# State-space scan: decay matrices written over their rows, rows fetched one head pair ahead, four DRAM copies of the rows instead of sixteen

## The chip, the cores and the metric

The kernel runs on one core of a Trainium2 chip. The metric is device time in microseconds, the median of the runs of one program. Of the core's engines the text speaks of TensorE (PE, matmuls; PEld is its weight load), VectorE (DVE), ScalarE (ACT), GpSimd (POOL) and SyncE (SP). SP computes nothing here: it issues nearly all transfers, one after the other, and a transfer whose target buffer is not free yet holds up everything behind it on SP. The transfers themselves are carried by 16 DMA engines.

## What is computed

The reference is an encoder of two layers on 512 tokens of width 1024. Each layer is a half-step feed-forward block, a token mixer and a second half-step feed-forward block, with layer norms between. The mixer of the first layer is a state-space mixer (Mamba-2 SSD) run in both directions; the change is in that mixer alone.

```python
proj = u @ w_in                       # z, xbc, dt_raw
xbc = silu(depthwise_conv(xbc, conv_w, conv_b))
dt = softplus(dt_raw + dt_bias);  A = -exp(a_log)
# per direction, 32 heads of 64 columns, 4 groups of B and C:
a_cs = cumsum(dt * A);  L = exp(segsum(a))          # decay matrix, per head
y_diag = einsum(C @ B^T, L, X * dt)
y_off  = C @ state * exp(a_cs)                      # what earlier tokens left
y = (y_f + y_b + X * d_skip) * silu(z);  y = rms_per_group(y) * norm_g
out = y @ w_out
```

## The kernel before

All matrix products in float32 are split into high and low parts and done as three matmuls; one *unit* is a 128x1024 block of weights (512 KB), loaded by SP into a `raw` buffer (`load`, L99), split by ACT (L123, `wh`) and DVE (L124, `wl`), and used by 24 matmuls of 512 columns (L166).

The state-space mixer is the function `ssm`. Its decay matrix for a head is exp(row + bias), where the row is the same for all 128 partitions and the bias is a column. So each head needs three rows of 512 numbers, spread over all partitions. `dt_chain` computes all rows once, as tiles `rows` and `rowe`, and writes them to a DRAM tile `scr` of shape [16, 32, 3, 512]: 16 equal copies of 32 heads times three rows (L667). `ssd_head` (one head) then fetches from it with two transfers: `rw`, two rows (L761, 128x1024, 512 KB in the tile), and `ch`, the third row (L763, 256 KB). The source pattern is 16 copies outermost, each read 8 times, so that partitions 0 to 7 get copy 0 and so on.

With `rw` there, POOL masks it (`mask`, L778) in place and into a second tile `dx`; `ssd_mats` makes the matrices of half of the tokens (`c` = 0 or 1): four exponentials on ACT (L786 to L789) into a tile `E` and into `dx`, an addition on POOL (L792) and a multiplication by `cb` on DVE (L793). DVE multiplies `ch` by C (L764). `ssd_out` then runs on PE (L803): for two heads, four products with `E` and two with `ch` for each half. In the trace each of these is two instructions, so a half is 8 and 4.

Two heads are a *pair*; there are 16 pairs, 4 in each of 4 groups, and each pair has two halves. Between the halves the main loop puts *units* of other work: the projections of the next group (`bc`, `x`), the gate (`z`) and the output projection of the group before (`wso`). Before the first group, `prepare` turns the group's B, C and x into the tiles `bt`, `cb`, `xt`, `st`.

Buffers: `rw` two, `E` five (which `dt_chain` also uses for its temporaries), `dx` two, `ch` three, `raw` four. The program is written in one order, and a scheduling layer arranges it for each engine by its own estimates of durations. Once built, the order on each engine is fixed, and an engine waits at its next instruction whatever stands behind it.

Of the kernel before, what the change touches and what calls it, by code (L numbers as in the profile page):

```python
# [9 lines left out]
F32 = mybir.dt.float32  # L10
F32R = mybir.dt.float32r
AF = mybir.ActivationFunctionType
ALU = mybir.AluOpType

P = 128
T = 512
# [2 lines left out]
FT = 22  # L19
FPARTS = (8, 7, 7)  # L20
NA = 32
NE = 5
NG = 4
NST = 128
ALPHA = 4.0 ** 0.25
EPS = 1e-5
# [20 lines left out]
def hybrid_trunk(tc, xT, cb, par, cst, adaw, wgu, wdn0, wdn1, wdn2, wdt, win, wso, wqk, wv, wao, dist_in, dtp, lam_in, out):  # L47
    nc = tc.nc
# [540 lines left out]
    def ssm(n):  # L589
        u = next_u[0]  # L590
        sc = ExitStack()
        ep = sc.enter_context(tc.tile_pool(name="ep", bufs=2))
# [6 lines left out]
        W = 256  # L599
        bias = ep.tile([P, 4, 64], F32, name="ssbias", bufs=1)  # L600
        dd = ep.tile([P, 4, 32], F32, name="dd", bufs=1)
        scr = dp.tile([16, 32, 3, T], F32, name="scr")

        def dt_proj():
            w = split(load(wdt, 512))
# [5 lines left out]
        def dt_chain(pd):  # L611
            dtT = tmp("dtT")
            nc.scalar.activation(dtT[:64], pd[:64], AF.Copy)
            pt = acc("ln")
            for i in range(4):
                nc.tensor.transpose(pt[:, i * 64 : (i + 1) * 64], dtT[:64, i * P : (i + 1) * P], ident[:64, :64])
            e1, e2, e3 = (ep.tile([P, T], F32, tag="E", name="E", bufs=NE) for _ in range(3))
            v, q, e, uu, lu = e1[:, :W], e1[:, W:], e2[:, :W], e2[:, W:], e3[:, :W]
            nc.vector.tensor_tensor(out=v, in0=pt[:, :W], in1=dtc[:, :W], op=ALU.add)
            nc.vector.scalar_tensor_tensor(out=q, in0=v, scalar=-1.0, in1=v, op0=ALU.mult, op1=ALU.max)  # L620
            nc.scalar.activation(e, q, AF.Exp, scale=-1.0)
            ea = e3[:, W:]
            nc.scalar.activation(ea, dtc[:, W:], AF.Exp)
            nc.vector.tensor_scalar(out=v, in0=v, scalar1=0.0, scalar2=None, op0=ALU.max)
            nc.vector.tensor_scalar(out=uu, in0=e, scalar1=1.0, scalar2=None, op0=ALU.add)
            nc.scalar.activation(lu, uu, AF.Ln)
            nc.vector.tensor_scalar(out=uu, in0=uu, scalar1=1.0, scalar2=None, op0=ALU.subtract)
            nc.vector.tensor_tensor(out=uu, in0=e, in1=uu, op=ALU.subtract)
            nc.vector.tensor_scalar(out=e, in0=e, scalar1=-0.5, scalar2=1.0, op0=ALU.mult, op1=ALU.add)
            nc.vector.tensor_tensor(out=uu, in0=uu, in1=e, op=ALU.mult)  # L630
            nc.vector.tensor_tensor(out=lu, in0=lu, in1=uu, op=ALU.add)
            nc.vector.tensor_tensor(out=v, in0=v, in1=lu, op=ALU.add)
            at = q
            nc.vector.scalar_tensor_tensor(out=at, in0=v, scalar=-1.0, in1=ea, op0=ALU.mult, op1=ALU.mult)
            nc.vector.tensor_scalar(out=v, in0=v, scalar1=1e-37, scalar2=None, op0=ALU.max)
            nc.scalar.activation(lu, v, AF.Ln)
            pcs = acc("ln")
            nones = tmp("nones")[:, :P]
            nc.gpsimd.memset(nones, -1.0)
            plan = {  # L640
                (0, 0): [(sgt, 0), (nones, 1)], (0, 1): [(sgt, 1)],
                (0, 2): [(sle, 2)], (0, 3): [(ones, 2), (sle, 3)],
                (1, 0): [(sge, 0), (ones, 1)], (1, 1): [(sge, 1)],
                (1, 2): [(slt, 2)], (1, 3): [(nones, 2), (slt, 3)],
            }
            for (dr, i), lst in plan.items():
                for k, (mk, j) in enumerate(lst):
                    nc.tensor.matmul(
                        pcs[:, i * 64 + dr * 32 : i * 64 + dr * 32 + 32], lhsT=mk,
                        rhs=at[:, j * 64 + dr * 32 : j * 64 + dr * 32 + 32],  # L650
                        start=k == 0, stop=k == len(lst) - 1,
                    )
            cs = tmp("cs")[:, :W]
            nc.scalar.activation(cs, pcs[:, :W], AF.Copy)
            nc.vector.tensor_tensor(out=bias.rearrange("p i h -> p (i h)"), in0=lu, in1=cs, op=ALU.subtract)
            pr = acc("ln")
            for i in range(4):
                nc.tensor.transpose(pr[:64, i * P : (i + 1) * P], cs[:, i * 64 : (i + 1) * 64], ident)
            rows = big(name="rows")
            nc.scalar.activation(rows[:64], pr[:64], AF.Copy)  # L660
            rowe = big(name="rowe")
            nc.scalar.activation(rowe[32:64, :W], pr[32:64, :W], AF.Exp)
            nc.scalar.activation(rowe[0:32, W:], pr[0:32, W:], AF.Exp)
            nc.scalar.activation(dd[:, 0:2, :], bias[:, 0:2, 0:32], AF.Exp)
            nc.scalar.activation(dd[:, 2:4, :], bias[:, 2:4, 32:64], AF.Exp)
            for j, a, b, src in ((0, 0, T, rows[0:32]), (1, 0, T, rows[32:64]), (2, 0, W, rowe[32:64]), (2, W, T, rowe[0:32])):
                nc.sync.dma_start(  # L667
                    scr[:, :, j, a:b].rearrange("r h x -> h r x"), src[:, a:b].unsqueeze(1).broadcast_to([32, 16, b - a])
                )

        last_in, last_exp = [None], [None]
# [44 lines left out]
        def prepare(g, xs, bc):  # L716
# [37 lines left out]
                states.append(st)  # L754
            return xt, cbs, states, Ct

        def ssd_head(h, Ct):

            src = scr[:, h].unsqueeze(1)
            rw = ep.tile([P, 2, T], F32, tag="rw", name="rw")  # L760
            nc.sync.dma_start(rw, src[:, :, 0:2].broadcast_to([16, 8, 2, T]))  # L761
            ch = ep.tile([P, T], F32, tag="ch", name="ch", bufs=3)
            nc.sync.dma_start(ch, src[:, :, 2].broadcast_to([16, 8, T]))  # L763
            nc.vector.tensor_tensor(out=ch, in0=ch, in1=Ct, op=ALU.mult)  # L764
            dx = ep.tile([P, 2, 2, P], F32, tag="dx", name="dx")
            f4 = rw[:, 0, :].rearrange("p (c o q) -> p c o q", c=2, o=2)
            b4 = rw[:, 1, :].rearrange("p (c o q) -> p c o q", c=2, o=2)
            for o, i_, fwd in (
                (f4[:, :, 0, :], f4[:, :, 0, :], True), (b4[:, :, 1, :], b4[:, :, 1, :], False),
            ):  # L770
                mask(o, i_, fwd)
            for o in range(2):
                mask(dx[:, :, o, :], (b4 if o == 0 else f4)[:, :, o, :], o == 1, inplace=False)
            return rw, ch, dx
# [6 lines left out]
            )  # L781

        def ssd_mats(h, c, rw, dx, cbs):
            E = ep.tile([P, T], F32, tag="E", name="E", bufs=NE)
            i = 2 * c
            nc.scalar.activation(E[:, :W], rw[:, 0, c * W : (c + 1) * W], AF.Exp, bias=bias[:, i, h : h + 1])  # L786
            nc.scalar.activation(E[:, W:], rw[:, 1, c * W : (c + 1) * W], AF.Exp, bias=bias[:, i + 1, 32 + h : 33 + h])
            nc.scalar.activation(dx[:, c, 0, :], dx[:, c, 0, :], AF.Exp, bias=bias[:, i, 32 + h : 33 + h])
            e = nc.scalar.activation(dx[:, c, 1, :], dx[:, c, 1, :], AF.Exp, bias=bias[:, i + 1, h : h + 1])  # L789
            last_exp[0] = e if h < 24 else None  # L790
            dg = E.rearrange("p (k q) -> p k q", k=4)[:, 0:4:3, :]
            nc.gpsimd.tensor_tensor(out=dg, in0=dg, in1=dx[:, c], op=ALU.add)  # L792
            nc.vector.tensor_tensor(out=E, in0=E, in1=cbs[c], op=ALU.mult)  # L793
            return E

        def ssd_out(pr_, c, py, mats, chs, xt, states):
            cc = slice(c * W, (c + 1) * W)
            col = [slice(pr_ * P + hh * 64, pr_ * P + (hh + 1) * 64) for hh in range(2)]
            for k in range(3):
                for hh in range(2):  # L800
                    lhs = xt[2 * c + k][:, col[hh]] if k < 2 else states[1 - c][:, col[hh]]
                    rhs = mats[hh][:, k * W : (k + 1) * W] if k < 2 else chs[hh][:, cc]
                    nc.tensor.matmul(py[hh * 64 : (hh + 1) * 64, cc], lhsT=lhs, rhs=rhs, start=k == 0, stop=k == 2)  # L803

        def gated_norm(g, ys, zs):
# [28 lines left out]
        def run(units):  # L834
            for f in units:
                f()
# [5 lines left out]
        run(units_x(0, xs, cols=HALVES)[:2])  # L842
        dt_chain(pd)
        run(units_x(0, xs)[2:])
        silu(bc + xs)
        scale_residual()
        run(units_z(0, zs[0])[:2])
# [9 lines left out]
        for g in range(NG):  # L857
# [7 lines left out]
            for s in range(8):  # L865
                pr_, c = divmod(s, 2)
                ft = g * 4 + pr_
                if c == 0:
                    heads = [ssd_head(ft * 2 + hh, Ct) for hh in range(2)]
                    py = acc("mid")  # L870
                mats = [ssd_mats(ft * 2 + hh, c, heads[hh][0], heads[hh][2], cbs) for hh in range(2)]
                ssd_out(pr_, c, py, mats, [hd[1] for hd in heads], xt, states)
                if c == 1:
                    nc.vector.scalar_tensor_tensor(
                        out=xs[pr_], in0=xs[pr_], scalar=pc(C_D + ft), in1=py, op0=ALU.mult, op1=ALU.add
# [321 lines left out]
```

## Time and profile before

| | |
|---|---|
| median of three runs | 2179.48 us (2178.3 to 2181.34) |
| the profiled execution's own time | 2176.88 us |
| its span, first to last instruction | 2174.8 us |
| PE busy | 97% |
| DVE busy | 82% |
| ACT, POOL busy | 50%, 7% |
| moved by DMA | 301.18 MB, mean 138 GB/s |
| the scan of the state-space mixer, first to last product of `ssd_out` | about 458 to 766 us |

Times are microseconds from the start of the span. A busy PE is not PE at its peak, since matmuls overlap; what counts are the stretches in which PE has nothing to do. A view of waits names the engine that waited, the line and tile of the waiting instruction, what it waited for, the total, the number of times and the longest. A row of the timeline has start, duration, engine, line, operation, output and inputs, count, and in brackets the idle time ahead of it. A row of stretches has, for each engine, busy time and instructions, then the granted clock of PE, the share of time in which the DMA engines were busy, and GB/s.

### The profile page before, as it was taken

How to read it: one execution, taken by the hardware profiler on the slowest of the kernel's cores; microseconds unless marked ns; L12 is line 12 of the kernel's file. 1: busy time of each engine (PE TensorE's matmuls, PEld its weight loads, DVE VectorE, ACT ScalarE, POOL GpSimd, SP SyncE). 2: the span in 40 equal slices, each digit the busy share in tenths (PEclk: the TensorE clock that was granted, in tenths of full speed). 3: DMA queues.
4: the chain of work that ended last, by engine and by line, in shares of the span. 5: the costliest groups of instructions: out<-in, count | busy, mean ns of one | idle time of the engine just before them, and what ended most of it. 6: DMA issues, size and time to landing. Idle time of an engine off the chain costs nothing.

```text
span 2174.8 us, 34198 instructions
## 1 busy us (share of the span) xinstructions
PE 2119.9 (97%) x13206; PEld 1859.7 (86%) x13206; DVE 1775.3 (82%) x3086; ACT 1092.4 (50%) x1828; POOL 154.2 (7%) x258
## 2 busy tenths in 40 slices
PE   7999999999999989999999999999999989999997
PEld 6889899866777778999999989899888869989897
DVE  6979899556766689989889998987877879858697
ACT  4424354767655546434356534343866637424353
POOL 0000000045232300000000000000111100000000
PEclk9999999999999999999999999999999989999999
DMA  9863644464535423646443273723322212323231
GB/s 324 302 212 121 219 138 149 123 183 137 158 123 155 121 68 126 214 144 198 159 132 105 97 261 96 254 94 111 98 80 79 76 59 78 127 69 117 84 110 39
DMA packets 90082, 301.18 MB, mean 138 GB/s; under 512 B 10048, under 2 KB 13504, under 8 KB 89920
## 3 DMA queue, kind: packets, MB, share of 16 engines
q1 hardware_dynamic: 88384, 294.81, 41.7%
q0 software_dynamic: 1536, 4.20, 0.9%
q8 instruction: 103, 1.69, 0.3%
q14 instruction: 59, 0.48, 0.1%
HBM read 289.53 MB, written 5.24 MB: 136 GB/s over the span
## 4 chain that ended last, share of the span: by engine, by line
PE 59%; DVE 3%; issue 2%; ACT 2%; POOL 1%; DMA 0%; POOLq 0%; ACTq 0%; DVEq 0%; SPq 0%
PE acc L166 47%; PE mid L166 9%; PE mid L965 1%; PE ln L166 1%; PE ln L987 0%; DVE resid L278 0%; DMA raw<-in_wgu 0%; DVE resid L320 0%; PE ln L253 0%; PE ln L302 0%; ACT p L975 0%; POOL E L792 0%; ACT wh L123 0%; PE ln L1004 0%; DVE p L968 0%
## 5 line engine op out<-in xcount | busy, mean ns | idle before, releaser
L166 PE MATMUL acc<-hi,wh 128*128 128x256 f32 (+1 forms) x1592 | 533.1, 336 | 9.2 <-DVE resid L372 7.1
L166 PE MATMUL acc<-hi,wl 128*128 128x256 f32 (+1 forms) x1592 | 532.6, 335 | 0.0
L166 PE MATMUL acc<-lo,wh 128*128 128x256 f32 (+1 forms) x1592 | 532.1, 335 | 0.1
L166 PE MATMUL acc<-uh,wh 128*128 128x256 f32 (+1 forms) x1160 | 391.2, 338 | 0.0
L166 PE MATMUL acc<-ul,wh 128*128 128x256 f32 (+1 forms) x1160 | 389.6, 336 | 0.0
L166 PE MATMUL acc<-uh,wl 128*128 128x256 f32 (+1 forms) x1160 | 388.9, 336 | 0.0
L123 ACT ACTIVATE wh<-raw 128x1024 fp32r<-128x1024 f32 (+1 forms) x210 | 212.8, 1021 | 277.5 <-PE acc L166 95.4
L166 PEld LDWEIGHTS acc<-hi,wh 128*128 128x128 f32 x1592 | 302.9, 190 | 45.5 <-DVE resid L372 6.6
L470 ACT ACTIVATE wh<-raw 128x1024 fp32r<-128x1024 f32 x198 | 209.1, 1059 | 259.4 <-DVE raw L480 129.1
L166 PEld LDWEIGHTS acc<-lo,wh 128*128 128x128 f32 x1592 | 302.9, 190 | 31.0 <-DVE lo L154 1.3
L166 PEld LDWEIGHTS acc<-hi,wl 128*128 128x128 f32 x1592 | 303.0, 190 | 30.3 <-issue 0.5
L124 DVE TENSOR_TENSOR wl<-raw,wh 128x1024 fp32r<-128x1024 f32 (+1 forms) x210 | 248.4, 1185 | 46.7 <-ACT wh L123 45.4
L471 DVE TENSOR_TENSOR wl<-raw,wh 128x1024 fp32r<-128x1024 f32 x198 | 240.8, 1219 | 38.9 <-ACT wh L470 38.1
L166 PEld LDWEIGHTS acc<-uh,wh 128*128 128x128 f32 x1160 | 219.0, 189 | 28.6 <-issue 6.2
L166 PEld LDWEIGHTS acc<-ul,wh 128*128 128x128 f32 x1160 | 219.3, 189 | 25.1 <-issue 3.2
L166 PEld LDWEIGHTS acc<-uh,wl 128*128 128x128 f32 x1160 | 219.2, 189 | 23.7 <-issue 2.4
L480 DVE TENSOR_TENSOR raw<-raw 128x512 f32<-128x512 f32 x264 | 181.3, 688 | 5.0
L184 DVE SCALAR_TENSOR_TENSOR raw<-raw,cond 128x1024 f32<-128x1024 f32 x144 | 174.1, 1218 | 9.9 <-DMA raw<-in_adaw 9.7
L372 DVE SCALAR_TENSOR_TENSOR resid<-acc,gv,resid 128x512 f32<-128x512 f32 (+1 forms) x166 | 109.4, 663 | 58.8 <-PE acc L166 58.4
L316 POOL TENSOR_TENSOR rr<-vr,mhalf 128x2 f32<-128x2 f32 x12 | 8.4, 698 | 1527.6 <-DVE vr L312 1527.6
L166 PE MATMUL mid<-uh,wh 128*128 128x256 f32 (+2 forms) x332 | 99.8, 302 | 0.0
L166 PE MATMUL mid<-uh,wl 128*128 128x256 f32 (+2 forms) x332 | 99.3, 299 | 0.0
(266 smaller groups left out, 3920.7 us busy)
## 6 DMA issues: line engine op xcount, KB each, us to landing
raw<-in_wgu SPq DMA_DIRECT2D x176, 512.0 KB, 4.2
raw<-in_adaw SPq DMA_DIRECT2D x144, 512.0 KB, 4.6
raw<-in_wdn SPq DMA_DIRECT2D x64, 448.0 KB, 4.0
raw<-in_win SPq DMA_DIRECT2D x40, 512.0 KB, 4.2
raw<-in_wdn SPq DMA_DIRECT2D x32, 512.0 KB, 4.4
rw<-scr SPq DMA_DIRECT2D x32, 512.0 KB, 5.5
ch<-scr SPq DMA_DIRECT2D x32, 256.0 KB, 3.6
raw<-in_wso SPq DMA_DIRECT2D x16, 512.0 KB, 3.5
```

Of the source, the lines that this page charges most:

```text
L123: nc.scalar.activation(hi[:, :n], raw, AF.Copy)
L124: nc.vector.tensor_tensor(out=lo[:, :n], in0=raw, in1=hi[:, :n].bitcast(F32), op=ALU.subtract)
L166: last = nc.tensor.matmul(o, lhsT=a, rhs=b, start=start and j == 0, stop=j == n - 1, skip_group_check=not start)
L184: nc.vector.scalar_tensor_tensor(out=raw, in0=raw, scalar=1.0, in1=cond, op0=ALU.mult, op1=ALU.mult, accum_out=mods[l][:, j : j + 1],)
L316: nc.gpsimd.tensor_tensor(out=r[:, :m], in0=vr[:, :m], in1=mhalf[:, :m], op=ALU.pow)
L372: nc.vector.scalar_tensor_tensor(out=res[d][:, a:b], in0=pd[:, a:b], scalar=gvec[n][:, d : d + 1], in1=res[d][:, a:b], op0=ALU.mult, op1=A ...
L470: nc.scalar.activation(x[0], r, AF.Copy)
L471: nc.vector.tensor_tensor(out=x[1], in0=r, in1=x[0].bitcast(F32), op=ALU.subtract)
L480: nc.vector.tensor_tensor(out=o, in0=x, in1=y, op=ALU.add)
L965: nc.tensor.matmul(ss[m], lhsT=q[:, c], rhs=qks[h, 1][m], start=j == 0, stop=j == 1)
```

## The change

- The tile `E` goes. `ssd_mats` writes the exponentials over the rows in `rw`, and the addition and multiplication work there too; `ssd_out` reads its matrices from `rw`. A row tile is thus held until the pair's last product and not only until its last exponential.
- `rw` has six buffers (`NRW`), and `dt_chain` takes two of them for its temporaries.
- The fetch of `rw` moves out of `ssd_head` into `fetch(ft)`, which the main loop calls for the next pair at the start of a pair, and for the first pair right behind the x projections of the first group. `ch` is fetched where it was.
- `scr` has 4 copies (`NREP`): L667 writes a quarter as much, and the source pattern of `rw` and `ch` is 4 copies outermost, each read 32 times.

```diff
-NE = 5
+NRW = 6
+NREP = 4
...
-        scr = dp.tile([16, 32, 3, T], F32, name="scr")
+        scr = dp.tile([NREP, 32, 3, T], F32, name="scr")
...
-            e1, e2, e3 = (ep.tile([P, T], F32, tag="E", name="E", bufs=NE) for _ in range(3))
+            e12, e3 = (ep.tile([P, 2, T], F32, tag="rw", name="ew", bufs=NRW) for _ in range(2))
+            e1, e2, e3 = e12[:, 0, :], e12[:, 1, :], e3[:, 0, :]
...
-                    scr[:, :, j, a:b].rearrange("r h x -> h r x"), src[:, a:b].unsqueeze(1).broadcast_to([32, 16, b - a])
+                    scr[:, :, j, a:b].rearrange("r h x -> h r x"), src[:, a:b].unsqueeze(1).broadcast_to([32, NREP, b - a])
...
+        rows_of = {}
+
+        def fetch(ft):
+            if ft >= 16:
+                return
+            for h in (2 * ft, 2 * ft + 1):
+                rw = ep.tile([P, 2, T], F32, tag="rw", name="rw", bufs=NRW)
+                nc.sync.dma_start(rw, scr[:, h].unsqueeze(1)[:, :, 0:2].broadcast_to([NREP, P // NREP, 2, T]))
+                rows_of[h] = rw
+
         def ssd_head(h, Ct):
-            src = scr[:, h].unsqueeze(1)
-            rw = ep.tile([P, 2, T], F32, tag="rw", name="rw")
-            nc.sync.dma_start(rw, src[:, :, 0:2].broadcast_to([16, 8, 2, T]))
+            rw = rows_of.pop(h)
             ch = ep.tile([P, T], F32, tag="ch", name="ch", bufs=3)
-            nc.sync.dma_start(ch, src[:, :, 2].broadcast_to([16, 8, T]))
+            nc.sync.dma_start(ch, scr[:, h].unsqueeze(1)[:, :, 2].broadcast_to([NREP, P // NREP, T]))
...
         def ssd_mats(h, c, rw, dx, cbs):
-            E = ep.tile([P, T], F32, tag="E", name="E", bufs=NE)
-            nc.scalar.activation(E[:, :W], rw[:, 0, c * W : (c + 1) * W], AF.Exp, bias=bias[:, i, h : h + 1])
-            nc.scalar.activation(E[:, W:], rw[:, 1, c * W : (c + 1) * W], AF.Exp, bias=bias[:, i + 1, 32 + h : 33 + h])
+            i, cc = 2 * c, slice(c * W, (c + 1) * W)
+            nc.scalar.activation(rw[:, 0, cc], rw[:, 0, cc], AF.Exp, bias=bias[:, i, h : h + 1])
+            nc.scalar.activation(rw[:, 1, cc], rw[:, 1, cc], AF.Exp, bias=bias[:, i + 1, 32 + h : 33 + h])
...
-            dg = E.rearrange("p (k q) -> p k q", k=4)[:, 0:4:3, :]
+            dg = rw.rearrange("p d (k q) -> p (d k) q", k=4)[:, i : i + 6 : 5, :]
             nc.gpsimd.tensor_tensor(out=dg, in0=dg, in1=dx[:, c], op=ALU.add)
-            nc.vector.tensor_tensor(out=E, in0=E, in1=cbs[c], op=ALU.mult)
-            return E
+            E = rw[:, :, cc]
+            nc.vector.tensor_tensor(out=E, in0=E, in1=cbs[c].rearrange("p (k q) -> p k q", k=2), op=ALU.mult)
...
-                    rhs = mats[hh][:, k * W : (k + 1) * W] if k < 2 else chs[hh][:, cc]
+                    rhs = rw[:, k, cc] if k < 2 else ch[:, cc]
...
         run(units_x(0, xs)[2:])
+        fetch(0)
         silu(bc + xs)
...
                 if c == 0:
+                    fetch(ft + 1)
                     heads = [ssd_head(ft * 2 + hh, Ct) for hh in range(2)]
```

The scheduling layer answers this with another order on the engines. The first place is SP, from the writing of the rows on. Before, `rw` and `ch` of a pair stand together, and three units of weights (`raw`) follow the first pair:

```order
L667 DMA scr<-rows 32x16x512 x2
L667 DMA scr<-rowe 32x16x256 x2
L761 DMA rw<-scr 128x1x1024 x2
L763 DMA ch<-scr 128x1x512 x3
L99 DMA raw<-in_win 128x1024 x3
L761 DMA rw<-scr 128x1x1024 x2
L763 DMA ch<-scr 128x1x512 x2
L99 DMA raw<-in_win 128x1024 x3
L761 DMA rw<-scr 128x1x1024 x2
```

Now, at the same place:

```order
L669 DMA scr<-rows 32x4x512 x2
L669 DMA scr<-rowe 32x4x256 x2
L766 DMA rw<-scr 128x1x1024 x4
L773 DMA ch<-scr 128x1x512 x2
L766 DMA rw<-scr 128x1x1024 x2
L773 DMA ch<-scr 128x1x512
L100 DMA raw<-in_win 128x1024 x3
L766 DMA rw<-scr 128x1x1024
L773 DMA ch<-scr 128x1x512
L766 DMA rw<-scr 128x1x1024
L773 DMA ch<-scr 128x1x512
L100 DMA raw<-in_win 128x1024 x2
```

Four row tiles stand ahead of the first `ch`, two more ahead of the third, and six row tiles and three `ch` ahead of the next weights. Behind the last row `rw`, `ch`, `rw`, `ch`, `raw` x2 follow twice more, so that eleven `rw`, seven `ch` and seven `raw` stand ahead of the eighth `ch`, which the fourth pair needs.

The second place is PE in `prepare` of the first group (`xd`, `bt`, `csts`, `xc` are its tiles, `acc` the units). Before, the piece below holds no product of `ssd_out`; the first of these stands behind 96 unit matmuls, counted from the first `ln<-xc` of `prepare`:

```order
L751 MATMUL ln<-xd,bt 128x512
L742 MATMUL ln<-csts,xc 128x128 x4
L166 MATMUL acc<-uh,wl 128x512
L166 MATMUL acc<-uh,wh 128x512
L166 MATMUL acc<-ul,wh 128x512
L166 MATMUL acc<-uh,wl 128x512
L742 MATMUL ln<-csts,xc 128x128 x4
L751 MATMUL ln<-xd,bt 128x512
```

Now the first product with a decay matrix (`rw`,`xt`) stands behind 13 unit matmuls:

```order
L753 MATMUL ln<-xd,bt 128x512
L744 MATMUL ln<-csts,xc 128x128 x4
L813 MATMUL mid<-rw,xt 64x256
L167 MATMUL acc<-ul,wh 128x512
L167 MATMUL acc<-uh,wl 128x512
L167 MATMUL acc<-uh,wh 128x512
L744 MATMUL ln<-csts,xc 128x128 x4
L167 MATMUL acc<-ul,wh 128x512
L813 MATMUL mid<-rw,xt 64x256 x2
L753 MATMUL ln<-xd,bt 128x512
L813 MATMUL mid<-rw,xt 64x256
```

In the first group the halves are now spread evenly: the first products with `ch` stand behind 38, 48, 96 and 144 unit matmuls for the four pairs, and the last product of the fourth pair behind 168, where it was 173 before. From the second group on PE has nearly the order it had.

More of the change, by code (lines that the diff above doesn't have):

```diff
@@ L783, in ssd_mats @@
         def ssd_mats(h, c, rw, dx, cbs):
-            E = ep.tile([P, T], F32, tag="E", name="E", bufs=NE)
-            i = 2 * c
-            nc.scalar.activation(E[:, :W], rw[:, 0, c * W : (c + 1) * W], AF.Exp, bias=bias[:, i, h : h + 1])
-            nc.scalar.activation(E[:, W:], rw[:, 1, c * W : (c + 1) * W], AF.Exp, bias=bias[:, i + 1, 32 + h : 33 + h])
+            i, cc = 2 * c, slice(c * W, (c + 1) * W)
+            nc.scalar.activation(rw[:, 0, cc], rw[:, 0, cc], AF.Exp, bias=bias[:, i, h : h + 1])
+            nc.scalar.activation(rw[:, 1, cc], rw[:, 1, cc], AF.Exp, bias=bias[:, i + 1, 32 + h : 33 + h])
             nc.scalar.activation(dx[:, c, 0, :], dx[:, c, 0, :], AF.Exp, bias=bias[:, i, 32 + h : 33 + h])
@@ L790, in ssd_mats, with ssd_out @@
             last_exp[0] = e if h < 24 else None
-            dg = E.rearrange("p (k q) -> p k q", k=4)[:, 0:4:3, :]
+            dg = rw.rearrange("p d (k q) -> p (d k) q", k=4)[:, i : i + 6 : 5, :]
             nc.gpsimd.tensor_tensor(out=dg, in0=dg, in1=dx[:, c], op=ALU.add)
-            nc.vector.tensor_tensor(out=E, in0=E, in1=cbs[c], op=ALU.mult)
-            return E
-        def ssd_out(pr_, c, py, mats, chs, xt, states):
+            E = rw[:, :, cc]
+            nc.vector.tensor_tensor(out=E, in0=E, in1=cbs[c].rearrange("p (k q) -> p k q", k=2), op=ALU.mult)
+        def ssd_out(pr_, c, heads, py, xt, states):
+            col = [slice(pr_ * P + hh * 64, pr_ * P + (hh + 1) * 64) for hh in range(2)]
             cc = slice(c * W, (c + 1) * W)
-            col = [slice(pr_ * P + hh * 64, pr_ * P + (hh + 1) * 64) for hh in range(2)]
             for k in range(3):
                 for hh in range(2):
+                    rw, ch, _ = heads[hh]
                     lhs = xt[2 * c + k][:, col[hh]] if k < 2 else states[1 - c][:, col[hh]]
-                    rhs = mats[hh][:, k * W : (k + 1) * W] if k < 2 else chs[hh][:, cc]
+                    rhs = rw[:, k, cc] if k < 2 else ch[:, cc]
                     nc.tensor.matmul(py[hh * 64 : (hh + 1) * 64, cc], lhsT=lhs, rhs=rhs, start=k == 0, stop=k == 2)
@@ L868, in ssm @@
                 if c == 0:
+                    fetch(ft + 1)
                     heads = [ssd_head(ft * 2 + hh, Ct) for hh in range(2)]
                     py = acc("mid")
-                mats = [ssd_mats(ft * 2 + hh, c, heads[hh][0], heads[hh][2], cbs) for hh in range(2)]
-                ssd_out(pr_, c, py, mats, [hd[1] for hd in heads], xt, states)
+                for hh in range(2):
+                    ssd_mats(ft * 2 + hh, c, heads[hh][0], heads[hh][2], cbs)
+                ssd_out(pr_, c, heads, py, xt, states)
                 if c == 1:
```

## The prediction

> **What bounds the kernel now.** I read the page first, then the waits of PE and of SP over the scan, then the transfers, then the timelines of PE and SP around the first pairs.
>
> ```profile
> span 2174.8 us, 34198 instructions
> PE 2119.9 (97%) x13206; PEld 1859.7 (86%) x13206; DVE 1775.3 (82%) x3086; ACT 1092.4 (50%) x1828; POOL 154.2 (7%) x258
> DMA packets 90082, 301.18 MB, mean 138 GB/s; under 512 B 10048, under 2 KB 13504, under 8 KB 89920
> q1 hardware_dynamic: 88384, 294.81, 41.7%
> ```
>
> PE has work 97% of the time, so a change in the scan gains at most what PE idles there, and loses as much as it makes PE idle. The waits of PE from 429 to 766 us, the scan with its lead-in:
>
> ```profile
> PE mid L803 <- DVE E L793: 4.7, 3, 3.6
> PE ln L751 <- DVE xd L747: 3.4, 4, 1.4
> PE mid L803 <- DVE ch L764: 1.1, 1, 1.1
> PE ln L742 <- ACT xt L744: 0.2, 1, 0.2
> ```
>
> Late decay matrices cost 4.7 us and a late `ch` 1.1 us; the other two rows belong to `prepare`, which the change leaves alone. The longest wait, and the granted clock behind it:
>
> ```profile
> 480.79 1.08 PE L803 MATMUL mid<-E,xt 128*64 128x256 f32 x2 [3.56 <-DVE E L793]
> 480.00:500.00 20.00, 18.49 (x81) 10.24 (x82) 14.60 (x20) 10.83 (x27) 9.57 (x17) 0.91 0.59 162
> ```
>
> After 3.56 us of idling the clock stands at 0.91 for the stretch, 9% of 20 us, or 1.8 us more. So all that a perfect fetch could win is 4.7 + 1.1 + 1.8 = 7.6 us, 0.35% of the time. SP's queue over the same stretch:
>
> ```profile
> SPq L763 <- PE mid L803: 68.7, 15, 9.9
> SPq L761 <- ACT E L787: 47.1, 20, 9.9
> ```
>
> `rw` waits 47.1 us for a free row tile, and that goes with six tiles. `ch` waits 68.7 us for the products of the pair before, since it has three buffers; that stays, and everything issued later on SP stands behind it.
>
> **The change, part by part.** *Matrices over rows.* The same exponentials, additions and multiplications run on as many elements. DVE's multiplication gets a pattern of 2x256 in place of 512; I cost it at nothing, since DVE has 18% to spare, and a longer one would show only if the matrix came last. The row tile is held until the pair's last product, but six tiles are three pairs, so the next holder is two pairs off.
>
> *Fewer bytes written.* The transfers in question, size and time to landing:
>
> ```profile
> raw<-in_wgu SPq DMA_DIRECT2D x176, 512.0 KB, 4.2
> rw<-scr SPq DMA_DIRECT2D x32, 512.0 KB, 5.5
> ch<-scr SPq DMA_DIRECT2D x32, 256.0 KB, 3.6
> raw<-in_wso SPq DMA_DIRECT2D x16, 512.0 KB, 3.5
> ...
> lam<-in_lam SPq DMA_DIRECT2D x1, 128.0 KB, 4.4
> ```
>
> ```profile
> 416.88 0.86 SPq L667 DMA_DIRECT2D scr<-rows  x2
> 417.79 4.64 SPq L667 DMA_DIRECT2D scr<-rowe  x2
> 429.01 2.99 SPq L761 DMA_DIRECT2D rw<-scr  x2
> ```
>
> The last write is issued by 422.4 and the first `rw` at 429.0. With a quarter of the bytes I let the first `rw` start at 426.5 (between 424.5, if little but the fixed time is left, and 429.0).
>
> *Four copies.* This part decides. All 25 rows of the list of transfers (its first and last stand above) add up to 628 issues, and there are 10048 packets under 512 B: 16 for each issue. So every transfer of this kernel, `rw` and `ch` with their 16 copies among them, ends in 16 small packets, one for each of the 16 DMA engines as I read it. I take it that a transfer is dealt out along the outermost dimension of its source: sixteen copies, one to an engine; four copies, four engines. No transfer before has an outermost dimension that 16 does not divide, so the trace does not show a smaller share; it is the forecast's one assumption.
>
> The Trainium skill, page "DMA: Bandwidth & Descriptors", section "Why a DMA increments its semaphore by 16 and not by 1", says the same: the number of engines is the largest up to 16 that divides the outermost dimension (other than 1) of both sides, and on this path they are the lowest-numbered ones. By that rule it was 16 before and is four now, the same four for every `rw` and `ch`. The trace agrees as far as 16 goes.
>
> Price per engine: GB/s over (busy share x 16), in three stretches:
>
> ```profile
> 548.00:551.20 3.20, 3.20 (x21) 1.96 (x20) 1.05 (x2) 2.24 (x6) 1.28 (x3) 1.00 0.77 283
> 560.00:562.00 2.00, 2.00 (x15) 1.24 (x16) 2.00 (x4) 1.60 (x5) 0.72 (x2) 1.00 0.54 215
> 460.00:480.00 20.00, 16.83 (x80) 10.65 (x76) 12.94 (x17) 11.13 (x28) 7.53 (x14) 1.00 0.88 234
> ```
>
> That is 23.0, 24.9 and, in a crowded stretch, 16.6 GB/s; the page's mean is 294.81 MB in 41.7% of 16 x 2174.8 us, 20.3 GB/s. Four engines move at most 100 GB/s together, so they are far from crowded: I take 23.0, with 24.9 and 20.3 as bounds. On four engines `rw` then takes 524,288 / (4 x 23,000) = 5.7 us of their time, `ch` 2.85, and a unit of weights (a sixteenth on each) 1.42.
>
> *The first group.* On SP eleven `rw`, seven `ch` and seven `raw` now stand ahead of the eighth `ch`, the one that the fourth pair needs for its first half. If the four engines serve them in order without a gap, that `ch` is through at 426.5 + 11 x 5.7 + 8 x 2.85 + 7 x 1.42 = 522. To landing another 2.1 us (3.5 of `raw<-in_wso` less its 1.4), and DVE's multiplication:
>
> ```profile
> 464.46 0.92 DVE L764 TENSOR_TENSOR ch<-ch,xc 128x512 f32<-128x512 f32 x1 [0.59 <-DMA ch<-scr]
> 461.58 0.40 PE L166 MATMUL acc<-uh,wl 128*128 128x512 f32 x1
> 461.81 0.40 PE L166 MATMUL acc<-uh,wh 128*128 128x512 f32 x1
> 548.48 1.08 PE L803 MATMUL mid<-E,xt 128*64 128x256 f32 x8
> 549.39 0.60 PE L803 MATMUL mid<-ch,st 128*64 128x256 f32 x4
> 498.88 0.80 PE L803 MATMUL mid<-ch,st 128*64 128x256 f32 x3
> ```
>
> so 525. Until then PE stands in front of that product, behind 144 unit matmuls; before, the fourth pair ended behind 173. The other 29 at 0.23 us and one half of 1.5 us make 8.2: PE is at 533 where it was at 499.7 (the last row). **+33 us**, in which the old waits of 4.7 us are already gone, since I compare ends. At 24.9 GB/s it is +26, at 20.3 +46. Queued behind these transfers on SP are the weights, but their PE work is held up longer by the same `ch`; DVE too stands at its `ch` multiplication with the splits of weights behind it, which I leave uncosted.
>
> *The other groups.* The scan ends here:
>
> ```profile
> 765.24 0.74 PE L803 MATMUL mid<-ch,st 128*64 128x256 f32 x3
> ```
>
> That is (766.0 - 499.7) / 12 = 22.2 us a pair. Four engines need 2 x 5.7 + 2 x 2.85 + 37/12 x 1.42 = 21.5: just enough in the mean, 2.2 us a pair too much at 20.3 GB/s (26 us), 2.3 us to spare at 24.9. Where pairs stand close there is a wait of its own: the second `ch` of a pair is issued when the pair before has ended, and lands 3.6 + 2.85 - 0.7 = 5.7 us later, or 11.4 with a `rw` ahead of it. In the last group there is this much time:
>
> ```profile
> 726.01 0.60 PE L803 MATMUL mid<-ch,st 128*64 128x256 f32 x4
> 733.14 0.60 PE L803 MATMUL mid<-ch,st 128*64 128x256 f32 x4
> ```
>
> 6.5 us from the end of one pair to the next `ch` product, so 0 to 5.7 us are missing for each of three pairs, and as much or less for the sixth pair. I take 3 us four times, and 2 for unevenness: **+14** (+8 and +37 at the bounds). The clock after long idle times once more, **+2**.
>
> The sum is +49 on the profiled execution's 2176.9 (span 2174.8 and 2.1 around it), 2226; the median of the runs is 2.6 above that execution, so **2228**. The bounds are +36 and +85.
>
> The same skill page, section "Where 436 GB/s comes from", gives 435 GB/s for 16 ports, an estimate of 27.2 GB/s per engine; the first group would lose 19 us by it and the whole some 26. The fastest stretch here shows 24.9.
>
> **The rivals.** *All sixteen engines still carry `rw` and `ch`* (not slower). Then the waits of 7.6 us go. Against that, PE meets the first pair's products behind 13 unit matmuls instead of 96, at about 436 us, while its first matrix was ready here:
>
> ```profile
> 447.16 0.69 DVE L793 TENSOR_TENSOR E<-E,cb 128x512 f32<-128x512 f32 x1 [2.58 <-POOL E L792]
> ```
>
> 2.5 us of earlier rows and a shorter queue make 441 to 443, so PE idles up to 7 us there: -7.6 to 0, I take -3, 2176. For it speaks that 16 packets per issue need not mean a split by the source's first dimension; against it, that the pattern's first number was exactly 16. It decides from six to seven engines on: 62 us for the sum above, in place of 95, bring PE to 499.7. Chance 0.12.
>
> *Four copies are slow to read as well.* Already `rw` lands later than `raw` of the same size (5.5 against 3.5 to 4.2), so reading one row again and again may hold an engine. At the crowded 16.6 GB/s the first group loses 70, and a pair needs 29.8 of 22.2 us, 91 more: some +174, 2353. Chance 0.08.
>
> *Forecast:* four engines at 20 to 25 GB/s, 0.80.
>
> **How the numbers follow.** The forecast alone gives 2215 to 2264. Below, with the earliest start and no later waits, it reaches 2203, and I go to 2198; above, a part of the slow-read case is taken in, to 2284. That leaves out the sixteen engines and the worst of slow reads, some 2 in 10. A measurement of this kernel can tell about 0.2%, 4.4 us, from no change. The sixteen engines, -7.6 to 0 about 2179.5, share their chance between faster (0.06) and same (0.06); slower keeps 0.88.
>
> **What would show it.** Right: 16 - 4 = 12 small packets fewer for each of 64 transfers, 9280 in place of 10048; `rw` landing at over 7.8 us; PE waiting tens of us at L813 for DVE's `ch`, above all in the second to fourth pair; a busy share near 0.25 to 0.4 while the queue is full. Wrong: 10048 small packets and `rw` at 4 to 6 us (all sixteen); long waits of PE spread over all groups (slow reads); waits for matrices rather than for `ch` (the order on POOL or ACT, not the queue, would be the cause).

## The result and the profile after

| | median, us | ratio to before, 95% interval |
|---|---|---|
| before | 2180.03 (2178.3 to 2181.34) | |
| changed | 2300.97 (2297.78 to 2302.8) | 1.0553 [1.054, 1.0567] |

The changed kernel is 5.5% slower, 121 us. The forecast was slower, 2228 us with a range of 2198 to 2284. The sign and the four engines hold; the size does not, and the measured time lies 17 us above the range.

The same lines of the page, after the change:

```profile
span 2301.0 us, 34177 instructions
PE 2154.2 (94%) x13206; PEld 1877.0 (82%) x13206; DVE 1771.7 (77%) x3086; ACT 1087.7 (47%) x1826; POOL 149.8 (7%) x258
DMA packets 87779, 298.83 MB, mean 130 GB/s; under 512 B 9280, under 2 KB 11968, under 8 KB 87616
q1 hardware_dynamic: 86080, 292.45, 38.1%
```

The span is 126 us longer with nearly the same instructions on each engine. The small packets are 9280, exactly the 10048 - 64 x 12 of the forecast: each `rw` and `ch` now ends in four of them. By its rule on the outermost dimension the Trainium skill, page "DMA: Bandwidth & Descriptors", section "Why a DMA increments its semaphore by 16 and not by 1", gives four engines for such a transfer. The trace agrees, with four packets in place of 16.

That four engines carry the rows, and how fast, is seen in stretches in which SP had just issued rows and little else was under way (columns as in the prediction: busy time of PE, PEld, DVE, ACT, POOL, then clock, DMA share, GB/s):

```profile
430.00:435.00 5.00, 5.00 (x26) 3.95 (x24) 2.19 (x3) 4.97 (x10) 2.70 (x5) 1.00 0.26 104
436.00:444.00 8.00, 0.66 (x5) 0.36 (x3) 0.00 (x0) 4.73 (x13) 1.15 (x4) 0.84 0.26 106
609.50:614.50 5.00, 5.00 (x24) 4.14 (x23) 5.00 (x9) 0.14 (x1) 0.00 (x0) 1.00 0.25 90
602.00:607.00 5.00, 5.00 (x29) 3.46 (x28) 3.10 (x4) 5.00 (x13) 2.04 (x3) 1.00 0.03 11
```

A share of 0.25 to 0.26 is 4 of 16 engines without a gap. GB/s over (share x 16) is 25.0, 25.5 and 22.5 for each engine in the first three rows, around the 23.0 of the forecast. `rw` and `ch` were under way together there, and the share stayed at a quarter, so the four are the same for both. The last row is the one to remember. At 602 us, in the second group, the same engines have nearly nothing to do: one burst of rows has landed, and the next is not issued yet. It is not the only gap: cut into slices of 2 us, the stretch from 542 to 894 us has 38 of 176 slices with a share under 0.1.

Where PE lost the time, in two stretches: up to the last product of the fourth pair, and from there to the last product of the scan. Before:

```profile
425.00:500.00 75.00, 70.28 (x322) 47.08 (x321) 42.70 (x55) 42.80 (x92) 28.73 (x50) 0.98 0.72 188
500.00:766.00 266.00, 261.28 (x1268) 192.28 (x1266) 177.35 (x238) 170.26 (x335) 89.95 (x146) 1.00 0.45 134
```

After:

```profile
425.00:542.00 117.00, 77.67 (x321) 52.20 (x319) 41.85 (x53) 52.07 (x121) 43.14 (x71) 0.81 0.37 113
542.00:894.00 352.00, 289.91 (x1274) 207.54 (x1272) 176.26 (x241) 157.24 (x305) 71.14 (x125) 0.92 0.31 100
```

Length less busy time of PE is its idle time: 4.7 and 4.7 us before, 39.3 and 62.1 after. The rest of the 42 and 86 us is the same products running longer at a lower granted clock, 0.81 and 0.92. So of 128 us in the scan 92 are idling (35 in the first group, 57 behind it) and 36 are the clock (7 and 29).

Who waited for whom, from 420 to 900 us; first PE, then the other engines:

```profile
PE mid L813 <- DVE ch L774: 47.0, 10, 6.8
PE ln L753 <- DVE xd L749: 27.7, 8, 10.0
PE mid L813 <- DVE rw L803: 10.5, 2, 10.1
```

```profile
POOL rw L788 <- DMA rw<-scr: 248.8, 31, 22.8
ACT rw L795 <- POOL dx L788: 86.0, 15, 12.7
DVE ch L774 <- DMA ch<-scr: 143.5, 26, 11.7
SPq L100 <- DVE wl L125: 283.1, 32, 19.8
```

PE waits mostly at `ch`, as forecast. The other rows matter more. POOL's mask waits for its rows 31 times, ACT's exponentials wait for the mask, and SP waits 283 us in front of weight loads for DVE's `wl`. One round of that, in the chain of waits of the second group:

```profile
582.93 16.93 DMA rw<-scr
...
600.35 0.41 POOL rw L788
600.76 0.37 POOL dx L788
601.15 0.40 ACT rw L796
...
606.39 0.80 POOL rw L801
607.19 0.38 SPq L766
...
608.27 16.19 DMA rw<-scr
```

A row tile needs 16.9 us from issue to landing, on four engines that it shares with the transfers issued along with it. Then come mask, exponentials and an addition, and only at 607 does SP issue the next rows; these need 16.2 us again. The chain enters SP by a short wait for that addition; a far longer one stands right in front of it. SP's wait from 586 to 607.2 us, and the rows of ACT and DVE behind it:

```profile
SPq L100 <- DVE wl L125: 17.8, 1, 17.8
```

```profile
601.15 0.51 ACT L796 ACTIVATE rw<-rw,ssbias 128x256 f32<-128x256 f32 x1 [7.70 <-POOL dx L788]
...
604.17 1.04 ACT L124 ACTIVATE wh<-raw 128x1024 fp32r<-128x1024 f32 x1
605.36 1.22 DVE L125 TENSOR_TENSOR wl<-raw,wh 128x1024 fp32r<-128x1024 f32 x1
```

SP stood 17.8 us at a weight load that needed a `raw` buffer, to be freed by the split of an earlier unit. That split stood on ACT (604.17) behind the exponentials, which had waited 7.7 us for the mask of the late rows. So the ring closes: rows, mask, exponentials, weight split, weight load, next rows. The rows of this round are those of the eighth pair, whose first product stands at 639.6 us, so for PE they come early enough. They come late for POOL and ACT, where their masks and exponentials stand ahead of other work. Before some fetches SP waits for something else: for the last products of a pair, which free a row tile (L766 for PE's `mid` of L813, 48.1 us in 8 waits).

### The profile page after: what moved, and what is told of

Its sections match the earlier page's. It is cut to its first block, busy times and chain, and to the rows that moved or that the text cites. A ratio compares the mean times of both kernels' runs of the same rounds, so it can differ in the third digit from the quotient of the medians.

```text
span 2301.0 us, 34177 instructions
## 1 busy us (share of the span) xinstructions
PE 2154.2 (94%) x13206; PEld 1877.0 (82%) x13206; DVE 1771.7 (77%) x3086; ACT 1087.7 (47%) x1826; POOL 149.8 (7%) x258
## 2 busy tenths in 40 slices
DMA packets 87779, 298.83 MB, mean 130 GB/s; under 512 B 9280, under 2 KB 11968, under 8 KB 87616
## 4 chain that ended last, share of the span: by engine, by line
PE 72%; DMA 13%; DVE 8%; ACT 3%; issue 2%; SPq 1%; POOL 1%; POOLq 0%; ACTq 0%; DVEq 0%
PE acc L167 58%; PE mid L167 9%; DMA rw<-scr 5%; DMA ch<-scr 4%; PE mid L978 1%; DVE raw L185 1%; PE mid L813 1%; DVE wl L125 1%; PE ln L167 1%; DMA raw<-in_wdn 1%; DMA raw<-in_adaw 1%; DMA raw<-in_win 1%; ACT wh L124 1%; SPq L773 1%; DVE raw L481 1%
## 5 line engine op out<-in xcount | busy, mean ns | idle before, releaser
L167 PE MATMUL acc<-uh,wh 128*128 128x256 f32 (+1 forms) x1160 | 396.2, 342 | 0.0
L185 DVE SCALAR_TENSOR_TENSOR raw<-raw,cond 128x1024 f32<-128x1024 f32 x144 | 174.4, 1222 | 10.8 <-DMA raw<-in_adaw 10.4
L774 DVE TENSOR_TENSOR ch<-ch,xc 128x512 f32<-128x512 f32 x32 | 23.7, 744 | 143.7 <-DMA ch<-scr 143.5
```

The costliest lines, as they stand in the source:

```text
L167: last = nc.tensor.matmul(o, lhsT=a, rhs=b, start=start and j == 0, stop=j == n - 1, skip_group_check=not start)
L185: nc.vector.scalar_tensor_tensor(out=raw, in0=raw, scalar=1.0, in1=cond, op0=ALU.mult, op1=ALU.mult, accum_out=mods[l][:, j : j + 1],)
```

## The experiments

The expectations name theories by letters. In the first runs A is "four engines", B "the new order", C "a few DRAM rows read too often", and A1 the prediction's account of the later groups, that a late `ch` is the link.

**Copies inside.** Four copies as in the change, and the order on every engine the same, but the source pattern has the 32 repeats outermost:

```diff
-scr[:, h].unsqueeze(1)[:, :, 0:2].broadcast_to([NREP, P // NREP, 2, T])
+scr[:, h].unsqueeze(0)[:, :, 0:2].broadcast_to([P // NREP, NREP, 2, T])
```

and the same for `ch`.

> The changed kernel with its four copies, but with the source pattern of rw and ch turned round: 32 repeats outermost, the four copies inside. The order on every engine is that of the changed kernel, and as much is written and read. Theory A (four copies outermost put each transfer on four of the 16 engines, and that is the whole loss): 10048 small packets, rw landing in 4.5 to 6 us, 2172 to 2182 us. Theory B (the new order on SP, with row tiles ahead of the third buffer's worth of ch, loses by itself): the order is the same, so still well above 2200 us. Theory C (few copies read again and again are slow to read): 10048 small packets, but rw landing in over 8 us and about 2300 us.

Measured: 2175.38 us, ratio 0.9978 [0.9969, 0.9987]. Its packets and landings:

```profile
DMA packets 88547, 298.84 MB, mean 137 GB/s; under 512 B 10048, under 2 KB 12736, under 8 KB 88384
rw<-scr SPq DMA_DIRECT2D x32, 512.0 KB, 5.9
ch<-scr SPq DMA_DIRECT2D x32, 256.0 KB, 5.8
```

Turning one pattern round takes away the whole loss, with the same bytes from the same four copies and the same order everywhere. A holds; B and C fall.

**Sixteen copies, the rest of the change kept** (`NREP = 16`).

> The changed kernel with sixteen copies again, outermost as before. Theory A: 10048 small packets, within 5 us of the run with four copies inside, 2172 to 2184 us. Theory B: above 2200 us. Theory C: 2172 to 2184 us. The full writing of the rows comes back, which I put at 0 to 4 us.

Measured: 2187.23 us, ratio 1.0042 [1.0027, 1.0056], with 10048 small packets. That is above the 2172 to 2184 expected. Matrices over rows and the fetch ahead do not pay by themselves; here they go with 0.4% more, 7.6 us, and the runs do not say which of the two it is. The full writing was put at 0 to 4 us. It costs more at its place: the first `rw` goes out at 429.35 us here and at 421.17 with four copies inside.

**Before, with four copies outermost only.**

```diff
-        scr = dp.tile([16, 32, 3, T], F32, name="scr")
+        scr = dp.tile([4, 32, 3, T], F32, name="scr")
...
-            nc.sync.dma_start(rw, src[:, :, 0:2].broadcast_to([16, 8, 2, T]))
+            nc.sync.dma_start(rw, src[:, :, 0:2].broadcast_to([4, 32, 2, T]))
```

and the write and `ch` alike.

> The kernel before with four copies, outermost, and nothing else: no fetch ahead, two row tiles, E kept. Theory A: 9280 small packets; a pair's two rw and two ch take some 17 us on four engines where they took 7, and are asked for only when the pair before has let its tiles go: 2240 to 2340 us. Theory B: 2178 to 2190 us, since the order of before is kept nearly. Theory C: as A in time.

Measured: 2304.21 us, ratio 1.0576 [1.0559, 1.0593]. So the four copies alone make the loss. The rest of the change wins back little of it, if anything: the medians are 3 us apart, and the intervals overlap.

**`ch` fetched ahead with `rw`**, in four buffers, four copies outermost:

```diff
                 nc.sync.dma_start(rw, scr[:, h].unsqueeze(1)[:, :, 0:2].broadcast_to([NREP, P // NREP, 2, T]))
+                ch = ep.tile([P, T], F32, tag="ch", name="ch", bufs=4)
+                nc.sync.dma_start(ch, scr[:, h].unsqueeze(1)[:, :, 2].broadcast_to([NREP, P // NREP, T]))
-                rows_of[h] = rw
+                rows_of[h] = rw, ch
```

> The changed kernel, four copies outermost, with ch fetched a pair ahead together with rw (four ch buffers in place of three). Theory A1 (the loss is a ring: ch lands late, DVE stands at its multiplication with the splits of weights behind it, SP stands at the weights with the next pair's transfers behind them, so a pair's transfers and its work follow each other): with ch early the ring opens, and the four engines need some 21.5 us of 22.2 a pair: 2190 to 2250 us. Theory A2 (the four engines are simply full): no gain, 2285 to 2310 us.

Measured: 2308.51 us, ratio 1.0597 [1.0579, 1.0615]. PE's longest waits there:

```profile
PE ln L753 <- DVE xd L749: 37.9, 9, 8.2
PE ln L723 <- ACT xc L715: 34.1, 3, 14.8
PE acc L167 <- ACT wh L124: 13.3, 8, 3.4
```

PE has no wait for `ch` left, and the kernel is no faster. The time went to `prepare` and to the weights. A1, the prediction's account of the later groups, falls: `ch` is where PE stood, not why. The time is the one that A2, full engines, gives, but they are not full: of the 180 slices of 2 us from 540 to 900 us, 49 have a DMA share under 0.1. The chain of waits shows the same ring without `ch`: a `rw` issued at 601.5 lands after 18.6 us, then come mask, exponentials, `wh`, `wl` and a weight load, and the next `rw` starts at 630.1.

**Rows issued by ACT**, the kernel of the run before with `nc.scalar.dma_start` for `rw` and `ch`, so that SP carries only weights.

> Four copies outermost, rw and ch both fetched a pair ahead (four ch buffers), and both issued by ACT in place of SP; the weights stay on SP. Theory A1 (a ring through SP: a pair's transfers are issued behind weights that wait for a raw buffer, the buffer waits for a split, and the split stands on ACT or DVE behind the pair's own rows): the rows no longer stand behind the weights, the ring is cut, and four engines need 21.5 us of 22.2 a pair: 2190 to 2250 us, still 9280 small packets. Theory A2 (the four engines are full): 2285 to 2310 us, as with ch ahead on SP.

Measured: 2318.85 us, ratio 1.0652 [1.0638, 1.0667], above both ranges. The two long waits of SP and ACT:

```profile
SPq L100 <- DVE wl L125: 448.5, 44, 30.5
ACT rw L795 <- POOL dx L788: 140.3, 18, 16.7
```

The rows no longer stand behind the weight loads, but the next fetch now stands on ACT behind exponentials that wait for the rows before: in the chain a `rw` lands at 623.4, mask and exponential follow, and ACT issues the next `rw` at 628.7. The ring closes through another queue.

**Eight copies outermost** (`NREP = 8`).

> The changed kernel with eight copies, outermost. Theory A: eight engines, 8 small packets per row transfer (9536 in all); a pair's transfers take 17 less 2 of fixed time halved, so some 9.5 us; the ring then has 8 us less per pair than with four copies, 16 pairs: 2300 less 100 to 125 us, 2176 to 2205 us. If the share did not follow the number of copies one by one: as with sixteen (2187 us) or as with four (2301 us).

Measured: 2213.94 us, ratio 1.0176 [1.0158, 1.0194], above what was expected; 9536 small packets, eight for each. From its fourth pair's end to its last product, and below it the same for sixteen copies:

```profile
506.00:804.00 298.00, 273.83 (x1274) 198.50 (x1274) 177.82 (x243) 157.33 (x306) 68.63 (x124) 0.97 0.37 118
500.00:778.00 278.00, 264.49 (x1272) 194.03 (x1270) 180.23 (x242) 160.62 (x313) 82.36 (x126) 0.99 0.44 126
```

By the prediction's sum eight engines need 2 x 2.85 + 2 x 1.42 + 4.4 (its three units of weights a pair) = 13 of 22.2 us a pair. Yet PE idles 24 us here, against 13.5 with sixteen copies and 9 with four copies inside (shown after the next two runs), and its clock is 0.97. In this kernel and in the one with sixteen copies the order on the engines differs a little from that of the changed kernel, so 13.5 is the fairer measure. A lack of rate in the mean does not explain the rest.

**Before, with four copies inside only**, and **four copies inside with `ch` ahead.**

> The kernel before with four copies read with the 32 repeats outermost, so 16 engines and a quarter of the writing, and nothing else of the change. If the 4 us that the changed kernel gains with its copies inside come from the shorter writing alone: 2173 to 2177 us. If they come from the six row tiles and the early fetch: 2178 to 2182 us.

> The changed kernel with the four copies inside (16 engines), and ch fetched a pair ahead as well, four ch buffers. PE waits 1.8 us for ch and 1.0 for matrices in the scan with the copies inside, so there is little left: 2171 to 2176 us. If the early ch pushes the weights back on SP: 2176 to 2185 us.

Measured: 2171.34 us, ratio 0.997 [0.9961, 0.998], and 2170.25 us, ratio 0.9964 [0.9952, 0.9977], both a little below what was expected. Fewer copies, with the pattern the right way round, are the part of the change that pays: the first of the two has nothing else of it. Whether it is the shorter writing or the turned pattern is not separated, since sixteen copies with the repeats outermost were not run. For comparison, the later groups with copies inside, the first kernel of this section:

```profile
494.00:766.00 272.00, 262.93 (x1273) 192.89 (x1271) 179.74 (x242) 156.37 (x303) 81.80 (x124) 1.00 0.40 129
```

**Rows issued by POOL**, `nc.gpsimd.dma_start`, else as the ACT run. Here S says that pairs alternate with the work that waits for them, and R that four engines are too slow in the mean.

> Four copies outermost, ch fetched ahead as in the fourth experiment, and all rw and ch issued by POOL, so that SP carries only weights during the scan; POOL is 7% busy, and each fetch stands on it up to a pair ahead of its use. Theory S (pairs alternate: the fetch of the next pair is gated by work that itself waits for the rows, so that the four engines idle between bursts; the gate lies in what is queued around the fetch): with the gate gone from SP and ACT most of the later groups' loss should go, 2200 to 2260. Theory R (four engines are simply too slow for 16 pairs, at whatever moment the transfers are issued): 2285 or more. If POOL's queue deals a transfer out over more engines, the small packets do not drop to 9280, the run comes out at 2190 or below, and it says nothing about S and R.

Measured: 2361.34 us, ratio 1.0839 [1.0823, 1.0854]. Its second queue, the landing of `rw`, and POOL's longest wait:

```profile
q0 software_dynamic: 27136, 29.46, 5.9%
...
rw<-scr POOLq DMA_DIRECT2D x32, 512.0 KB, 10.4
```

```profile
POOL rw L766 <- issue: 155.4, 15, 13.2
```

POOL's queue is of another kind, with many more packets, and POOL itself stands in front of the fourth transfer of a pair (its second `rw`), up to 13.2 us, with masks and additions behind it. The time lies in R's range, but with this queue in place of the other the run says nothing on S and R: inconclusive.

**One copy, 128 repeats outermost**, without and with `ch` ahead (`NREP = 1`, pattern as in the first experiment).

> The changed kernel with a single copy of the rows in DRAM and the 128 repeats outermost: all sixteen engines read the same few kilobytes. If the number of copies matters only through the number of engines: 10048 small packets and 2168 to 2180, no slower than four copies with 32 repeats outermost (2175.4). If one copy is a hot spot for reading: rw lands well above 6 us and the time is above 2190.

> As the run before, with ch fetched ahead beside rw. If copies matter only through engines: 2165 to 2174, about the 2170.3 of four copies with repeats outermost and ch ahead, or a little below since still less is written. If one copy is a hot spot: above 2185.

Measured: 2171.55 us, ratio 0.9967 [0.9954, 0.9979], and 2168.67 us, ratio 0.9956 [0.9942, 0.9969]. The second:

```profile
rw<-scr SPq DMA_DIRECT2D x32, 512.0 KB, 5.8
ch<-scr SPq DMA_DIRECT2D x32, 256.0 KB, 5.8
scr<-rows SPq DMA_DIRECT2D x2, 64.0 KB, 1.7
scr<-rowe SPq DMA_DIRECT2D x2, 32.0 KB, 1.6
```

One copy of the rows, read by all sixteen engines at once, lands as fast as four. Copies in DRAM are not needed in this kernel. This version has the lowest time of the study and beats both kernels, by 0.4% the one before; its interval overlaps with those of one copy without `ch` ahead and of four copies with it.

**Only `ch`, and only `rw`, with copies outermost.** The other has its repeats outermost, and the order on every engine is that of the changed kernel. In these expectations C is again "`ch` is the link".

> The changed kernel with the copies outermost for ch alone; rw has its 32 repeats outermost, and the order on every engine is that of the changed kernel. Service time that a pair adds on the four engines, at the prediction's 23 GB/s: 2 x (2.85 - 0.71) = 4.3 us in place of 12.8. Theory S (pairs alternate with the work that waits for them; in the changed kernel and with eight copies about half of the added service time stays uncovered, 6.6 of 12.8 and 2.1 of 4.3 us a pair): as eight copies, 12 x 2.1 = 25 us in the later groups and some 12 in the first, 2205 to 2225. Theory R (only a lack of rate in the mean; the four engines need about 13 of 22.2 us a pair here): no loss in the later groups, 2176 to 2190. Theory C (ch is the link, whatever rw does): most of the loss stays, above 2240.

> The other half: copies outermost for rw alone, ch with its repeats outermost, same order on every engine. Added service time 2 x (5.7 - 1.42) = 8.6 us a pair. Theory S: 12 x 4.3 = 51 us in the later groups and 25 to 35 in the first, 2240 to 2270. Theory R (about 17 of 22.2 us needed a pair): a loss in the first group alone, 2185 to 2210. Theory C (ch is the link): 2176 to 2215.

Measured: 2197.71 us, ratio 1.0081 [1.0066, 1.0096], and 2289.06 us, ratio 1.0506 [1.0488, 1.0523]. Only `ch`, then only `rw`, from the fourth pair's end to the last product:

```profile
506.00:790.00 284.00, 268.04 (x1273) 195.72 (x1272) 176.87 (x241) 156.08 (x302) 75.66 (x123) 0.99 0.40 124
```

```profile
534.00:874.00 340.00, 287.54 (x1278) 206.36 (x1275) 180.26 (x243) 157.97 (x306) 78.49 (x125) 0.92 0.33 103
```

Against the 272 us with both on sixteen engines, `ch` adds 12 us and `rw` 68, and both together, in the changed kernel, 80. In these executions the two add up; the one with only `rw` is the fastest of its kernel, 8.6 us below the median, so the sum can be off by as much. C falls: it is `rw` that carries the loss. R falls with the second run, where four engines would need 17 of 22.2 us a pair and 68 us are lost all the same. S is left, but not with its numbers. The first time is below its range and the second above: not half of the added time stays uncovered, but 68 / 12 = 5.7 of 8.6 us a pair for `rw` and 1.0 of 4.3 for `ch`. The chain of the second run shows why `ch` is late there too, in a kernel that reads `ch` with all engines:

```profile
599.97 14.69 DMA ch<-scr
...
615.36 1.42 DVE wl L125
...
620.95 0.96 ACT wh L124
621.93 1.24 DVE wl L125
623.18 0.33 SPq L100
...
623.61 0.54 SPq L766
624.20 0.02 SPq L773
624.25 11.72 DMA ch<-scr
```

A `ch` issued behind two `rw` takes 14.7 us, against 5.8 in the first experiment. I read it as the part of `ch` that falls on the four engines having to wait there for `rw`. And the weight split stands between one fetch and the next, as in the changed kernel.

## Why the prediction was wrong in size

*What bounds the kernel, and the mechanism.* Right as to the engines. The first experiment differs from the changed kernel by the order of two dimensions and loses nothing. The assumption that a transfer is dealt out by the outermost dimension of its source is borne out by 4, 8 and 16 small packets for 4, 8 and 16. Of the signs named, the packets, `rw` landing far above 7.8 us and PE standing at DVE's `ch` all came; but only 18.9 of its 47.0 us at `ch` fell to the first four pairs, where they were expected above all. DVE's multiplication in place, costed at nothing, took 0.69 us as before. Two smaller steps failed: the wait of `rw` for a row tile, 47.1 us before, did not go with six tiles (48.1 us, now for PE's products), and PE's wait for `xd` of `prepare`, which the change was to leave alone, went from 3.4 to 27.7 us.

*Fewer bytes written.* The first `rw` went out at 421, 5.5 us earlier than taken and outside the bounds of 424.5 to 429, to the good side.

*Price per engine.* 23.0 GB/s was taken, 22.5 to 25.5 measured. That is not why the forecast was too low.

*The first group, +33 us.* Near in size, but partly by luck. The fourth pair ended at 542.1, and with the five unit matmuls that then still stood behind it and not ahead (1.2 us) that is +43.6, inside the bound of +46. PE idled 35 us more there; the rest is the clock. But the step behind the number, that the four engines serve the queue "in order without a gap", did not hold. SP stood at weight loads until 517 us, and the eighth `ch` went out only then:

```profile
518.54 12.40 DMA ch<-scr
```

It landed at 530.9. From the measured start of the first `rw`, 421, the forecast's own sum gives 421 + 95.4 + 2.1 = 518.5, so the queue took 12 us longer than the sum; from 468 to 475 us the DMA share was 0.01. That the rows started 5.5 us early hid part of it. Of the 39.3 us of idling 18.9 are waits for `ch`, 10.5 for the first matrices and 10.0 for `xd`.

*The other groups, +14 us.* This step failed. The sentence was "just enough in the mean": 21.5 us needed of 22.2 a pair, with a wait of 3 us at four places. It takes for granted that the four engines are never without work while a pair passes. They were without work, at a DMA share of 0.03 between two bursts, because the next transfers are issued only when work is done that itself waits for the rows: a pair takes 29.3 us, not 22.2. (The 37 units of weights in that sum are 34 on SP's queue, which makes 21.1 and changes nothing.) The idle time of PE behind the first group is 57 us more than before. That it isn't the mean rate is shown by eight copies, and by `rw` alone outermost. That `ch` isn't the link is shown by fetching it ahead, and by `rw` alone outermost.

*The clock, +2 us.* This failed too, as a term of its own. I had priced it once, from one idle time of 3.56 us. PE now waited ten times for `ch` alone, and the granted clock was 0.81 over the first group and 0.92 over the rest, and PE's busy time grew by 36 us. More than a quarter of the loss is not idling but slow products.

Put together: +35 and +57 of idling and +36 of clock, 128 us at the end of the scan, 126 in the span, 121 between the medians. The forecast had 33, 14 and 2.

*The rivals.* Sixteen engines: out, by 9280 packets. Slow reading: out, by 22.5 to 25.5 GB/s for each engine, and one copy lands as fast as four. That its 29.8 us a pair is near the measured 29.3 is chance, and its +174 is 13 more than the 70 and 91 it names. Its sign of recognition, waits spread over all groups, did appear, for another reason. I had written that this pattern would mean slow reads; it was the wrong reading to commit to.

*What stays open.* The ring is shown in the chains of four kernels (the changed one, `ch` ahead, rows issued by ACT, only `rw` outermost), for single rounds; how much of the 57 us each way of closing it costs was not measured. That cutting it, with four engines kept, would give back most of the 57 us was not shown: from ACT the fetch stood behind exponentials, and from POOL it met another kind of queue. Exponentials put behind the weight splits on ACT were not tried. Why the changed kernel with sixteen copies is 0.4% slower than before stays open too; its first `rw` goes out at nearly the same time (429.35 against 429.01).

## What to carry to other kernels

When a broadcast is read from DRAM, write the source pattern with a dimension outermost that 16 divides (here the 32 or 128 repeats) and count the small packets of a transfer in the profile: 4 and 8 in place of 16 went with 4 and 8 engines here. A balance of bytes and rate in the mean doesn't say that a fetch is hidden; follow one round, from the landing of one fetch through the work that waits for it to the issue of the next, and ask on which queue it closes. And where PE will be made to wait again and again, cost the slower clock behind each wait as well as the wait.

## What the runs showed of the hardware

- Four engines that carried rows alone gave 90 to 106 GB/s, 22.5 to 25.5 GB/s each. A DRAM row read many times was no hot spot: one copy for all 128 partitions landed in 5.8 us, four copies in 5.9.
- A `ch` dealt out over all sixteen engines took 14.7 us behind two `rw` on four of them, against 5.8 where all were on sixteen.
- The same fetches through POOL's queue took 10.4 us for `rw` and left 28481 packets under 512 B in place of 9280, with POOL held up to 13.2 us at an issue.
- Fewer copies shortened the writing ahead of the scan more than expected: one copy landed in 1.7 us (`scr<-rows`) and 1.6 (`scr<-rowe`), sixteen copies in 9.2 and 14.4.
